# Two-layer encoder trunk on one core: accumulating transfers planned later, four products moved among the first retention tiles, and a ring of its own for results

## The chip, the core and the metric

The kernel runs on one core of one Trainium2 chip. The metric is the device time of one execution in microseconds (us). Three runs of the kernel before took 1896.23, 1899.14 and 1902.46 us, so the median is 1899.14 us. The execution under the profiler took 1899.7 us; the span from its first to its last instruction is 1897.9 us, and its mean granted TensorE clock is 0.988.

Engines are called as the profile calls them: PE (TensorE matmul), PEld (its weight loads), DVE (VectorE), ACT (ScalarE), POOL (GpSimd) and SP (SyncE, which issues most transfers).

## What is computed

Two groups of 512 rows of width 1024 pass the same two layers and a final norm. Layer 0 is differential attention, layer 1 is bidirectional retention. The change lies where layer 1's projections end, and in retention itself:

```python
def bidir_retention(h, w_in, decay_fwd, decay_bwd, subln_g, w_out):
    proj = h @ w_in
    q, k, v, gate = jnp.split(proj, [RET_QK_WIDTH, 2 * RET_QK_WIDTH, 2 * RET_QK_WIDTH + D_INNER], axis=-1)
    q = retention_rotate(q.reshape(B, S, N_HEADS, RET_QK_DIM))
    k = retention_rotate(k.reshape(B, S, N_HEADS, RET_QK_DIM)) * (RET_QK_DIM ** -0.5)
    ...
    o = rms_norm(o_f + o_b, subln_g, SUBLN_EPS)
    o = o.reshape(B, S, D_INNER) * jax.nn.silu(gate)
    return o @ w_out
...
x = x + bidir_retention(h, ret_w_in[j], ret_decay_fwd[j], ret_decay_bwd[j], ret_subln_g[j], ret_w_out[j])
...
return rms_norm(x, final_norm_g, NORM_EPS)
```

There are 8 heads; a head's output is 256 wide. Matrices are float32, and each matmul is made as three passes over a high and a low part (`PASSES`).

## The kernel before

**Plan.** Each operation is recorded by `plan.op` with its engine, an assumed cost and what it reads and writes. `Plan.arrange` then walks through an assumed course of the five engines and fixes one order for each. An operation becomes ready when the last one it depends on is done; of the ready ones an engine takes the most urgent. The order is fixed in the program, so on the chip each engine takes its instructions strictly in that order, and an instruction that waits holds everything behind it on its engine.

**Projections.** Both layers' input projections and retention's output projection are made by a seven-product scheme: P1, P2, P5, P6, P3, P7, P4 (`SEQ`) stand for the eight block products of a 2 by 2 matrix product. A `Unit` of the second projections ("pair") makes seven such products of 12 matmuls each (line 623); `projections` is a generator that gives one product per step. The products collect in three kinds of PSUM banks, x, y and z; z lies in the two banks tagged `sc`, which the retention scores use as well.

**Retention.** It runs over 16 blocks (head and group) of 4 tiles of 128 rows, 64 tiles in all, here called tile 0 to tile 63. Block after block, a tile takes these steps:

- a *score* of the next block (three matmuls, line 1222). DVE multiplies it with the decay table F (line 1226) and ACT and DVE split it into high and low part (lines 433 and 436).
- *av*: 12 matmuls into one of the two banks tagged `o` (line 1240).
- the *norm*: ACT squares and sums the result (line 785), two small POOL operations make the factor (lines 789 and 790), and ACT applies it (line 799).
- the *turn*: two PE transposes into the same bank (line 805), after which DVE multiplies with the gate (line 1291) and the bank is free for the tile after next.

On PE, av of tile i+1 stands ahead of the turn of tile i, and the turn of tile i ahead of av of tile i+2. As a tile is turned, `fill` puts two products of the output projection (`out2`, line 1347, six matmuls each) between.

**Output projection.** For each pair of heads p (0 to 3) and group g there are 14 products: seven for each of two row blocks r. For p below 3, `evac_add` forms 256 KB results in tiles tagged `out`, and `dma_add` (line 1262) adds them to the residual rows in DRAM with an accumulating transfer on POOL's queue: 48 such *pieces* (`x` in the profile). For the last p, `evac_last` adds in on-chip memory, and half sums and the final norm follow.

**Weights of the next pair.** `w_split` makes the seven operands while the second group of a pair runs. P1, P2 and P3 are loaded by SP. P5, P6 and P4 add a further 512 KB block onto P1's place `wa`, and P7 adds one onto P3's place `wb`, each with an accumulating transfer on POOL's queue: 16 such *weight blocks* (`b<-in_ret_w_out_dram` on POOL). They are called W5, W6, W7 and W4 here. Each can go only when the operand before it on its place is split (ACT line 433, DVE line 436, 128 by 1024), and is itself split when it has landed. The first pair's blocks go at the end of the projections (the *junction*); the other three sets at the three *boundaries* between pairs.

So POOL's one queue holds the small norm operations of all tiles, the weight blocks and the pieces, in one fixed order.

**Places.** Score products (`rt`), results (`out`) and the scratch of the half sums (`jk`) all take the next of eight 512-wide tiles e0 to e7 in turn. `LATE` names places for retention by hand; `turns` goes round such a list.

Of the kernel before, what the change touches and what calls it, by code (L numbers as in the profile page):

```python
# [15 lines left out]
P = 128  # L16
# [13 lines left out]
ENGINES = ("PE", "ACT", "DVE", "POOL", "SP")  # L30
PASSES = ((0, 0), (0, 1), (1, 0))
WS_BUFS = 7
LAG = 4


# [32 lines left out]
class Plan:  # L68
# [6 lines left out]
    AHEAD = 15.0  # L75

    def __init__(self):
        self.rings, self.state, self.ops, self.places = {}, {}, [], []

    def op(self, eng, cost, fn, r=(), w=(), lands=0.0, kb=0, load=False):  # L80


        n = len(self.ops)
        costs = eng if isinstance(eng, dict) else {eng: cost}
        preds, order = set(), set()
        for keys, writes in ((r, False), (w, True)):
            keys = [key if isinstance(key, tuple) else (key, None) for key in keys]
            for thing, part in keys:
                parts = self.state.setdefault(id(thing), {"thing": thing})
                if isinstance(thing, Buf):  # L90
                    if thing.nth + thing.bufs < len(thing.ring):
                        late = thing.ring[thing.nth + thing.bufs]
                        assert late.first is None, f"{thing.tag} {thing.nth} is used after its place was taken"
                    if thing.first is None:
                        assert writes, f"{thing.tag} is read before it is written"
                        thing.first = n
                        if thing.nth:
                            before = thing.ring[thing.nth - 1].first
                            assert before is not None, f"{thing.tag}: places are taken out of turn"
                            order.add(before)  # L100
                        if thing.nth >= thing.bufs:
                            preds.update(thing.ring[thing.nth - thing.bufs].users)
                        if thing.at:
                            lo, hi = thing.at
                            for b in [b for b in self.places if b.at[0] < hi and lo < b.at[1]]:
                                preds.update(b.users)
                                b.taken = True
                                self.places.remove(b)
                            self.places.append(thing)
                    elif thing.first != n:  # L110
                        assert not thing.taken, f"{thing.tag} {thing.nth} is used after its place was taken"
                        order.add(thing.first)
                    thing.users.append(n)
                for q, entry in parts.items():
                    if q == "thing" or not (part is None or q is None or q == part):
                        continue
                    if entry[0] is not None:
                        preds.add(entry[0])
                    if writes:
                        preds.update(entry[1])  # L120
                if writes:
                    if part is None:
                        for q in [q for q in parts if q != "thing"]:
                            del parts[q]
                    parts[part] = [n, []]
                else:
                    parts.setdefault(part, [None, []])[1].append(n)
        preds.discard(n)
        order -= preds
        self.ops.append((costs, fn, sorted(preds), sorted(order), lands, kb, load))  # L130
        return n

    def arrange(self, starts):
# [42 lines left out]
        while len(out) < n_ops:  # L176
            best = None
            for e in ENGINES:
                while soon[e] and (done[soon[e][0][1]] or soon[e][0][0] <= free[e]):
                    _, n = heapq.heappop(soon[e])  # L180
                    if not done[n]:
                        heapq.heappush(avail[e], (place[n] if e == "PE" else late[n], n))
                while avail[e] and done[avail[e][0][1]]:
                    heapq.heappop(avail[e])
                at = None
                if avail[e] and not (e == "PE" and avail[e][0][0] > head + self.WINDOW):
                    at = free[e]
                    if e == "SP" and ops[avail[e][0][1]][6] and avail[e][0][0] + drift - self.AHEAD > at:
                        at = avail[e][0][0] + drift - self.AHEAD
                        if soon[e]:  # L190
                            at = min(at, soon[e][0][0])
                elif soon[e]:
                    at = soon[e][0][0]
                if at is not None and (best is None or at < best[0]):
                    best = (at, e)
            assert best is not None, "stuck"
            at, e = best
            if at > free[e]:
                free[e] = at
# [12 lines left out]
            if e == "PE":  # L212
                drift = at - starts[n]
                while head < len(pe) and done[pe[head]]:
                    head += 1
            for s in succs[n]:
                same = not kb and e in ops[s][0] and len(ops[s][0]) == 1
                after = at + cost if same else end
                if n in ops[s][3]:
                    after = at  # L220
                ready[s] = max(ready[s], after)
                left[s] -= 1
                if not left[s]:
                    known(s)
# [24 lines left out]
def trunk_kernel(  # L249
# [75 lines left out]
    def place(name, shape, dt=F32, size=1024, pool=None):  # L325
# [3 lines left out]

        def make(i):  # L330
            t = (pool or wk).tile([P, size], dt, tag=name, name=label, bufs=1)
            return shaped(t[0:shape[0], 0:n], shape)
        return Buf(plan, name, 1, make, lambda i: where(name))

    def late(kind, i, shape, dt=F32):

        name = LATE[kind][i]
        if isinstance(name, int):
            return slot(name, shape, dt)
        return place(name, shape, dt, 512 if name[0] in "cm" else 1024)  # L340

    def turns(kind, shape, dt=F32):

# [5 lines left out]
    LATE = dict(q0=["raw0"], k0=["raw1"], v0=["raw2", "raw3"], aT0=["st0", "st1", "st2", "os0"], sg0=["os1"], F0=["os2"],  # L349
                aT1=[0, 1, 2, 3], k1=[4], q1=[5], v1=[6, 7], AB=[8, 9, 10], sg1=[12], F1=[13], wa=[20], wb=[21], S4=[22],  # L350
                w=[11, 14, 15, 16, 17, 18, 19, "ws5", "ws6", 23, 24, 25, 26, 27],
                AS=["ws0", "ws1", "ws2", "ws3", "ws4"], O=["m0", "m1", "m2"], R=["m3", "c3"],
                x=[20, 21, "raw0", "raw1", "raw2", "raw3", "os1", "os2"])

    def const(shape, tag, dt=F32):
        return Buf(plan, tag, 1, lambda i: view(cp, tag, i, math.prod(shape[1:]), shape, dt), lambda i: where(tag))
# [186 lines left out]
    class Unit:  # L543
        def __init__(self, w, c0, kind, done, view=None):
# [4 lines left out]
            self.wide = kind == "wide"  # L549
            self.n_ws = 2 if self.wide else 1  # L550
            self.early = None
            self.ops, self.x, self.s = {}, {}, {}
            self.banks = {}

# [55 lines left out]
        def product(self, op):  # L610
# [1 line left out]
            n_banks = 2 if self.wide else 1  # L612
            opens = op in OPENS
            if opens:
                self.banks[which] = [bank(dict(x="pj", z="sc", y="o")[which], which) for _ in range(n_banks)]
            a, b = self.ops.pop(op), B_OF[op]
            bt = [Bop[b, k] for k in range(4)]
            reads = [q[1] for q in a] + bt
# [545 lines left out]
    tab2 = load_tab(rot_tab)  # L1164
    second_units = units2(tab2)
    step(made, 4)
    proj = projections(second_units, 12)
    step(proj, 6)
    run(made)
    run(proj)  # L1170


    blocks = [(2 * p + i, g) for p in range(NH // 2) for g in range(NG) for i in range(2)]
# [41 lines left out]
    def score2(b, j):  # L1215
# [5 lines left out]
            for i, (u, v) in enumerate(PASSES):  # L1221
                nc.tensor.matmul(s.t, k[:, u, j * P:(j + 1) * P], q[:, v, :], start=(i == 0), stop=(i == 2))  # L1222
        pe(0.7, fn, [q, k], [s])
        t1 = e_t("rt")
        F = Fs[h]
        dve(S, lambda: nc.vector.tensor_tensor(t1.t, s.t, F[:, 384 - P * j:896 - P * j], op=ALU.mult), [s, F], [t1])  # L1226
        aT = late(f"aT{b % 2}", j, [P, 2, S], F32R)
# [30 lines left out]
    wop, R_, AB, AS, O2, xh, banks = {}, {}, {}, {}, {}, {}, {}  # L1258
    wa = {}

    def dma_add(out, in_, r, w, kb):
        plan.op("POOL", 1.0, lambda: nc.gpsimd.dma_start(out(), in_(), accum_op=ALU.add), r, w, lands=5.5, kb=kb)  # L1262

    def w_block(p, e, i):
        return wo2[p * S:(p + 1) * S, i * S:(i + 1) * S].rearrange("(h e p) c -> p h e c", h=2, e=2)[:, :, e, :]
# [97 lines left out]
    def evac_add(g, r, op, ps):  # L1363
# [4 lines left out]
            return c  # L1368

        def put(c, alu, t, i):  # L1370
            e = e_t("out")
            dve(S, lambda: nc.vector.tensor_tensor(e.t, c.t, ps.t, op=alu), [c, ps], [e])
            add_to(g, t, i, lambda: e.t, [e])
        if op in ("P1", "P5", "P6"):
# [5 lines left out]
        elif op == "P7":  # L1380
            put(kept["P5"], ALU.subtract, 2 + r, 1)
        else:
            e = e_t("out")
            act(S, lambda: nc.scalar.copy(e.t, ps.t), [ps], [e])
            add_to(g, 2 + r, 0, lambda: e.t, [e])

    def half_sum(g, t, i):
        ss, jk, x = col(1, "ssf", 4), e_t("jk"), xh[g, t]
        act(S + 120, lambda: nc.scalar.activation(jk.t, x[:, i * S:(i + 1) * S], AF.Square, accum_out=ss.t),
            [(x, i)], [jk, ss])  # L1390
        halves.setdefault((g, t), []).append(ss)
# [38 lines left out]
    N2 = len(tiles2)  # L1430
    owed.clear()
    fetch_sg(0)
    for op in SEQ:
        w_split(0, op)
    for j in range(NT):
        score2(0, j)
    paid = 0
    for i in range(N2 + 2):
        if i < N2:
            b, t = tiles2[i]  # L1440
            if b + 1 < NB:
# [72 lines left out]
```

## Time and profile before

| | before |
|---|---|
| median of three runs | 1899.14 us |
| profiled execution | 1899.7 us |
| its span | 1897.9 us |
| DVE busy | 1463.5 us (77%) |
| ACT busy | 966.7 us (51%) |
| POOL busy | 226.6 us (12%) |
| transfers, mean | 172 GB/s |

The second projections end at about 1525 us, and retention fills the rest. A row of the timeline gives the start, the duration, the engine, the line and the operation, then the tile written and read, and in brackets how long the engine had been idle before it and what ended that. A row of the table of windows gives, for a stretch, each engine's busy time with its count of instructions, the granted TensorE clock (1.00 is full), the share of the DMA engines' time, and GB/s. A row of transfers gives their count, the size and the time from issue to landing.

### The profile page before, as it was taken

Reading aid. Unit: us, or ns where it says so; the run is one execution under the profiler, and the core shown is the slowest. Engines: PE = TensorE matmul, PEld = TensorE weight load, DVE = VectorE, ACT = ScalarE, POOL = GpSimd, SP = SyncE. Lnnn points to the kernel's source line nnn. Section 1 sums busy time; section 2 is a strip of 40 time slices with the busy share of each in tenths; the row PEclk is TensorE's granted clock in tenths of the full one; section 3 lists DMA queues with packets and bytes.
Section 4 is the critical chain, followed back from the end, with each engine's and each line's share of the span. In section 5 each row is a group of like instructions: output and inputs, shape, how many; then the busy total and the mean of one; then the engine's idle time right before and its main releaser. Section 6 shows DMA issues by size and latency. Waiting matters only on the chain. (4 is left out here: it accounts for less than half of the span.)

```text
span 1897.9 us, 27938 instructions
## 1 busy us (share of the span) xinstructions
PE 1819.4 (96%) x10241; PEld 1569.4 (83%) x10241; DVE 1463.5 (77%) x2451; ACT 966.7 (51%) x1973; POOL 226.6 (12%) x436
## 2 busy tenths in 40 slices
PE   6999999999999899999999999999999979797987
PEld 5888988989889788888888788989898958686866
DVE  7979688688788588888887978685858477576667
ACT  6634443443444465555556754343434356455553
POOL 2000000000000011111112100000000023334332
PEclk9999999999999999999999999999999989999999
DMA  4435535545455774444453244544444688879883
GB/s 157 125 119 180 179 119 183 162 130 170 151 160 163 275 277 173 159 158 166 178 178 120 103 133 133 179 151 160 145 160 144 220 251 224 212 215 201 238 201 120
DMA packets 161025, 326.18 MB, mean 172 GB/s; under 512 B 13028, under 2 KB 73080, under 8 KB 160888
## 3 DMA queue, kind: packets, MB, share of 16 engines
q1 hardware_dynamic: 149440, 303.36, 47.9%
q0 software_dynamic: 11264, 20.98, 6.8%
q8 instruction: 80, 1.31, 0.3%
q14 instruction: 57, 0.47, 0.1%
q10 hardware_dynamic: 184, 0.08, 0.0%
HBM read 202.72 MB, written 121.63 MB: 171 GB/s over the span
## 5 line engine op out<-in xcount | busy, mean ns | idle before, releaser
L623 PE MATMUL bank<-arena,ws 128*128 128x512 f32 x2160 | 514.4, 392 | 4.9 <-DVE e L491 3.0
L623 PEld LDWEIGHTS bank<-arena,ws 128*128 128x128 f32 x2160 | 404.1, 188 | 92.9 <-ACT ws L433 3.0
L623 PE MATMUL bank<-b,ws 128*128 128x512 f32 x1200 | 293.7, 392 | 2.4 <-DVE e L660 2.4
L623 PEld LDWEIGHTS bank<-b,ws 128*128 128x128 f32 x1200 | 224.6, 188 | 51.7 <-DVE e L660 2.2
L436 DVE TENSOR_TENSOR ws<-st,ws 128x512 fp32r<-128x512 f32 (+1 forms) x192 | 147.8, 774 | 90.8 <-ACT ws L433 59.2
L652 ACT COPY c<-bank 128x512 f32<-128x512 f32 x168 | 98.2, 585 | 213.5 <-PE bank L623 134.4
L630 PE MATMUL bank<-ws,arena 128*128 128x256 f32 x1728 | 204.0, 276 | 0.0
L630 PEld LDWEIGHTS bank<-ws,arena 128*128 128x128 f32 x1728 | 201.0, 188 | 1.4
L874 PE MATMUL bank<-ws,arena 128*128 128x512 f32 x768 | 202.0, 400 | 0.0
L436 DVE TENSOR_TENSOR ws<-raw,ws 128x512 fp32r<-128x512 f32 (+1 forms) x156 | 127.4, 822 | 77.9 <-ACT ws L433 69.1
L433 ACT CAST ws<-st 128x512 fp32r<-128x512 f32 (+1 forms) x192 | 131.9, 693 | 98.5 <-PE bank L623 57.3
L789 POOL TENSOR_SCALAR css<-css 128x1 f32<-128x1 f32 x128 | 47.2, 369 | 996.3 <-ACT bank L787 918.5
L874 PEld LDWEIGHTS bank<-ws,arena 128*128 128x128 f32 x768 | 139.5, 188 | 27.2 <-ACT m L418 0.2
L433 ACT CAST ws<-raw 128x512 fp32r<-128x512 f32 (+1 forms) x156 | 114.1, 738 | 75.5 <-PE bank L623 58.8
L660 DVE TENSOR_TENSOR e<-bank,c 128x512 f32<-128x512 f32 x168 | 115.1, 685 | 32.7 <-PE bank L623 28.3
L630 PE MATMUL bank<-ws,b 128*128 128x256 f32 x960 | 116.8, 276 | 0.0
L1073 ACT ACTIVATE b<-bank,nm 128x512 f32<-128x512 f32 x128 | 88.1, 688 | 50.5 <-DVE nm L1065 50.4
L630 PEld LDWEIGHTS bank<-ws,b 128*128 128x128 f32 x960 | 113.2, 188 | 0.7
L879 DVE TENSOR_TENSOR b<-bank,b 128x512 f32<-128x512 f32 x128 | 87.7, 685 | 31.1 <-PE bank L874 29.8
L1109 PE MATMUL bank<-arena 128*128 128x256 f32 x768 | 106.5, 288 | 0.0
L1057 PE MATMUL bank<-arena 128*128 128x512 f32 x384 | 100.6, 398 | 5.0 <-ACT b L1073 5.0
L1065 DVE TENSOR_REDUCE nm<-bank 128x1 f32<-128x512 f32 x128 | 86.6, 687 | 12.5 <-PE bank L1057 12.1
(156 smaller groups left out, 2832.1 us busy)
## 6 DMA issues: line engine op xcount, KB each, us to landing
qk<-os SPq DMA_DIRECT2D x192, 256.0 KB, 3.8
arena<-qk SPq DMA_DIRECT2D x80, 512.0 KB, 4.8
raw<-in_da_w_in_dram SPq DMA_DIRECT2D x64, 512.0 KB, 4.8
v<-os SPq DMA_DIRECT2D x64, 512.0 KB, 4.1
arena<-v SPq DMA_DIRECT2D x48, 512.0 KB, 4.2
raw<-in_ret_w_in_dram SPq DMA_DIRECT2D x48, 512.0 KB, 4.4
g<-e SPq DMA_DIRECT2D x48, 256.0 KB, 4.5
x<-e POOLq DMA_DIRECT2D x48, 256.0 KB, 6.7
```

Source lines behind the costliest of these rows:

```text
L433: act(n, lambda: nc.scalar.copy(dst(), src()), r, w)
L436: dve(n, lambda: nc.vector.tensor_tensor(dst(), src(), hi().bitcast(F32), op=ALU.subtract), r, w)
L623: nc.tensor.matmul(ps.t, a[u][0]()[:, k, :], bt[k][:, v, :], start=(opens and k == 0 and i == 0), stop=(k == 3 and i == 2), skip_group_che ...
L630: nc.tensor.matmul(ps[:, (t % 2) * 256:(t % 2) * 256 + 256], bt[k][:, v, t * P:(t + 1) * P], a[u][0]()[:, k, :], start=(opens and t % 2 == ...
L652: act(S, lambda c=c, ps=ps: nc.scalar.copy(c.t, ps.t), [ps], [c])
L660: dve(S, lambda e=e, ps=ps, c=c: nc.vector.tensor_tensor(e.t, ps.t, c.t, op=ALU.add), [ps, c], [e])
L874: nc.tensor.matmul(ps.t, o[a][:, e, t * P:(t + 1) * P], u[b][:, e, :], start=(n == 0), stop=(n == 5))
L879: dve(S, lambda: nc.vector.tensor_tensor(half, ps.t, half, op=ALU.add), [ps, (x, i)], [(x, i)])
L1057: nc.tensor.matmul(s.t, q[:, a, t * P:(t + 1) * P], k[:, b, :], start=(n == 0), stop=(n == 2))
L1065: dve(S, lambda s=s, m=m: nc.vector.tensor_reduce(m.t, s.t, op=ALU.max, axis=AX.X, negate=True), [s], [m])
L1073: act(840, lambda j=j, s=s, m=m: nc.scalar.activation(p[:, j, :], s.t, AF.Exp, bias=m.t, accum_out=sm[:, j:j + 1]), [s, m], [(p, j), (sm, j)])
L1109: nc.tensor.matmul(o[:, 0:256], aT[:, a, j * P:(j + 1) * P], v[b][:, j, :], start=(n == 0), stop=(n == 11))
```

## The change

It has three parts.

1. `dma_add` carries `hold=5.0`: in the plan's assumed course an accumulating transfer is ready only 5 us after what it depends on. The 5 us is in no instruction: on the chip there is only the order that follows from it.
2. `LEFT = 4`: the last four products of the last unit (P6, P3, P7, P4) are recorded among the first retention tiles, and the first pair's `w_split` behind them. The last unit's z bank is the one tagged `tp` in place of `sc`.
3. Score products take turns over e0 to e2 and results over e3 to e7, and a few other places are exchanged: `O`, `R` and the order in `x`, where the last pair's residual rows lie.

```diff
@@ Plan
-    def op(self, eng, cost, fn, r=(), w=(), lands=0.0, kb=0, load=False):
+    def op(self, eng, cost, fn, r=(), w=(), lands=0.0, kb=0, load=False, hold=0.0):
...
+        if hold:
+            self.holds[n] = hold
...
-                ready[s] = max(ready[s], after)
+                ready[s] = max(ready[s], after + self.holds.get(s, 0.0))
@@ LATE
-                AS=["ws0", "ws1", "ws2", "ws3", "ws4"], O=["m0", "m1", "m2"], R=["m3", "c3"],
-                x=[20, 21, "raw0", "raw1", "raw2", "raw3", "os1", "os2"])
+                AS=["ws0", "ws1", "ws2", "ws3", "ws4"], O=["m1", "m2", "m3"], rt=["e0", "e1", "e2"], out=["e3", "e4", "e5", "e6", "e7"], R=["m0", "c3"],
+                x=["raw0", "raw1", 20, 21, "raw2", "raw3", "os1", "os2"])
@@ Unit
+            self.z = "sc"
...
-                self.banks[which] = [bank(dict(x="pj", z="sc", y="o")[which], which) for _ in range(n_banks)]
+                self.banks[which] = [bank(dict(x="pj", z=self.z, y="o")[which], which) for _ in range(n_banks)]
@@ trunk_kernel
+    second_units[-1].z = "tp"
...
-    run(proj)
+    step(proj, 7 * len(second_units) - 6 - LEFT)
...
-        t1 = e_t("rt")
+        t1 = turns("rt", [P, S])
...
-    def dma_add(out, in_, r, w, kb):
-        plan.op("POOL", 1.0, lambda: nc.gpsimd.dma_start(out(), in_(), accum_op=ALU.add), r, w, lands=5.5, kb=kb)
+    def dma_add(out, in_, r, w, kb, hold=5.0):
+        plan.op("POOL", 1.0, lambda: nc.gpsimd.dma_start(out(), in_(), accum_op=ALU.add), r, w, lands=5.5, kb=kb, hold=hold)
...
-            e = e_t("out")
+            e = turns("out", [P, S])
...
-    for op in SEQ:
-        w_split(0, op)
     for j in range(NT):
         score2(0, j)
-    paid = 0
     for i in range(N2 + 2):
+        if i < LEFT:
+            step(proj)
+        elif i == LEFT:
+            run(proj)
+            for op in SEQ:
+                w_split(0, op)
```

What it moves is seen in the engines' orders. In the rows of the changed kernel line 1268 is before's 1262, 794 and 795 are 789 and 790, 628 is 623, 1228 is 1222 and 810 is 805.

POOL at the first boundary, before. The rows are W5, two pieces, the norm of tile 21 (two rows), W6, the norm of tile 22, a piece, W7, a piece, and the first row of the norm of tile 23:

```order
L1262 DMA b_180_13757<-in_ret_w_out_dram 128x2x512
L1262 DMA x12_194<-e_0_432 128x512
L1262 DMA x11_193<-e_2_482 128x512
L789 TENSOR_SCALAR css_1_5427<-css_1_5427 128x1
L790 TENSOR_TENSOR crs_1_5439<-css_1_5427,mhalf_0_208 128x1
L1262 DMA b_180_13757<-in_ret_w_out_dram 128x2x512
L789 TENSOR_SCALAR css_2_5476<-css_2_5476 128x1
L790 TENSOR_TENSOR crs_2_5487<-css_2_5476,mhalf_0_208 128x1
L1262 DMA x11_193<-e_4_656 128x512
L1262 DMA b_191_13968<-in_ret_w_out_dram 128x2x512
L1262 DMA x13_195<-e_6_705 128x512
L789 TENSOR_SCALAR css_3_5531<-css_3_5531 128x1
```

The same place in the changed kernel, some rows further on: a piece, W7 (`b_231`), the norm of tile 24, W6 (`b_216`), two pieces, and the norm of tile 25:

```order
L1268 DMA x11_193<-b_234_14050 128x512
L1268 DMA b_231_14004<-in_ret_w_out_dram 128x2x512
L794 TENSOR_SCALAR css_0_5375<-css_0_5375 128x1
L795 TENSOR_TENSOR crs_0_5388<-css_0_5375,mhalf_0_208 128x1
L1268 DMA b_216_13784<-in_ret_w_out_dram 128x2x512
L1268 DMA x13_195<-b_239_14089 128x512
L1268 DMA x13_195<-b_244_14129 128x512
L794 TENSOR_SCALAR css_1_5427<-css_1_5427 128x1
L795 TENSOR_TENSOR crs_1_5439<-css_1_5427,mhalf_0_208 128x1
```

So W7 moved ahead of W6 and behind the norm of tile 23, with one norm between the two blocks, and W6 has two pieces right behind it. Ahead of these rows the changed order reads: a piece, W5, the norm of tile 21, two pieces, the norms of tiles 22 and 23. The same pattern stands at all three boundaries, on both sides.

POOL at the junction, in the changed kernel: the norm of tile 5, W7, the norm of tile 6, W6, the norm of tile 7. (Before, W5 stood ahead of every norm, W6 behind the norm of tile 2, W7 behind that of tile 3, and the norm of tile 4 behind W7.)

```order
L794 TENSOR_SCALAR css_1_5427<-css_1_5427 128x1
L795 TENSOR_TENSOR crs_1_5439<-css_1_5427,mhalf_0_208 128x1
L1268 DMA b_134_13096<-in_ret_w_out_dram 128x2x512
L794 TENSOR_SCALAR css_2_5476<-css_2_5476 128x1
L795 TENSOR_TENSOR crs_2_5487<-css_2_5476,mhalf_0_208 128x1
L1268 DMA b_131_12988<-in_ret_w_out_dram 128x2x512
L794 TENSOR_SCALAR css_3_5531<-css_3_5531 128x1
L795 TENSOR_TENSOR crs_3_5542<-css_3_5531,mhalf_0_208 128x1
```

W5 now stands behind the norm of tile 1 and W4 behind that of tile 10 (before: tile 5), so each weight block stands two to five tiles later.

PE at the junction, before: the end of P7, two scores, P4 (four rows that collect in `bank_2`), four scores.

```order
L623 MATMUL bank_2_393<-b_100_9427,ws_2_356 128x512 x3
L1222 MATMUL bank_4_303<-b_105_12810,b_106_12813 128x512 x3
L1222 MATMUL bank_3_289<-b_105_12810,b_106_12813 128x512 x3
L623 MATMUL bank_2_393<-b_101_9473,ws_3_408 128x512 x3
L623 MATMUL bank_2_393<-b_102_9489,ws_3_408 128x512 x3
L623 MATMUL bank_2_393<-b_103_9492,ws_3_408 128x512 x3
L623 MATMUL bank_2_393<-b_104_9495,ws_3_408 128x512 x3
L1222 MATMUL bank_4_303<-b_105_12810,b_106_12813 128x512 x3
L1222 MATMUL bank_3_289<-b_105_12810,b_106_12813 128x512 x3
L1222 MATMUL bank_4_303<-arena_75 128x512 x3
L1222 MATMUL bank_3_289<-arena_75 128x512 x3
```

In the changed kernel the first two scores stand ahead of P6, P3 and P7, and P4 stands behind av of tile 1 and one more score, ahead of the turns of tiles 0 and 1:

```order
L1228 MATMUL bank_3_289<-arena_75 128x512 x3
L628 MATMUL bank_2_393<-b_101_9473,ws_3_408 128x512 x3
L628 MATMUL bank_2_393<-b_102_9489,ws_3_408 128x512 x3
L628 MATMUL bank_2_393<-b_103_9492,ws_3_408 128x512 x3
L628 MATMUL bank_2_393<-b_104_9495,ws_3_408 128x512 x3
L810 MATMUL bank_5_282<-ident_0_212,on_0_206 128x128 x2
L810 MATMUL bank_6_296<-ident_0_212,on_1_5212 128x128 x2
```

Up to P5 of the last unit PE's order is the same in both kernels.

More of the change, by code (lines that the diff above doesn't have):

```diff
@@ L32 @@
 WS_BUFS = 7
+LEFT = 4
 LAG = 4
@@ L77, in __init__ @@
     def __init__(self):
-        self.rings, self.state, self.ops, self.places = {}, {}, [], []
-    def op(self, eng, cost, fn, r=(), w=(), lands=0.0, kb=0, load=False):
+        self.rings, self.state, self.ops, self.places, self.holds = {}, {}, [], [], {}
+    def op(self, eng, cost, fn, r=(), w=(), lands=0.0, kb=0, load=False, hold=0.0):
         n = len(self.ops)
@@ L331, in make @@
             t = (pool or wk).tile([P, size], dt, tag=name, name=label, bufs=1)
+            places.pop((name.rstrip("0123456789"), int(name.lstrip("abcdefghijklmnopqrstuvwxyz"))), None)
             return shaped(t[0:shape[0], 0:n], shape)
@@ L339, in late @@
             return slot(name, shape, dt)
-        return place(name, shape, dt, 512 if name[0] in "cm" else 1024)
+        return place(name, shape, dt, 512 if name[0] in "cme" else 1024)
     def turns(kind, shape, dt=F32):
@@ L1382, in evac_add @@
         else:
-            e = e_t("out")
+            e = turns("out", [P, S])
             act(S, lambda: nc.scalar.copy(e.t, ps.t), [ps], [e])
@@ L1387, in half_sum @@
     def half_sum(g, t, i):
-        ss, jk, x = col(1, "ssf", 4), e_t("jk"), xh[g, t]
+        ss, jk, x = col(1, "ssf", 4), turns("out", [P, S]), xh[g, t]
         act(S + 120, lambda: nc.scalar.activation(jk.t, x[:, i * S:(i + 1) * S], AF.Square, accum_out=ss.t),
```

## The prediction

> **What bounds the kernel now.** The page's first section says which engine to look at.
>
> ```profile
> PE 1819.4 (96%) x10241; PEld 1569.4 (83%) x10241; DVE 1463.5 (77%) x2451; ACT 966.7 (51%) x1973; POOL 226.6 (12%) x436
> ```
>
> PE is busy for 1819.4 of 1897.9 us, and the change neither adds nor removes a matmul. So it can only win or lose in PE's idle time, 78.5 us, and in time at a lowered clock. The table of windows over the stages that the change touches shows where that time lies.
>
> ```profile
> 1520.00:1550.00 30.00, 22.61 (x131) 18.37 (x129) 27.71 (x50) 20.90 (x44) 6.87 (x10) 1.00 0.94 297
> 1550.00:1570.00 20.00, 13.75 (x64) 12.21 (x65) 10.15 (x18) 11.30 (x26) 7.99 (x12) 0.66 0.67 164
> 1570.00:1630.00 60.00, 60.00 (x350) 52.24 (x349) 42.91 (x85) 35.84 (x87) 23.23 (x38) 1.00 0.82 221
> 1630.00:1660.00 30.00, 19.35 (x99) 15.55 (x98) 15.27 (x26) 12.71 (x28) 12.76 (x17) 0.89 0.91 210
> 1720.00:1750.00 30.00, 19.62 (x103) 15.81 (x102) 15.84 (x27) 13.29 (x29) 12.80 (x17) 0.89 0.94 210
> 1810.00:1840.00 30.00, 21.32 (x105) 16.72 (x104) 17.31 (x30) 14.23 (x31) 11.87 (x17) 0.91 0.85 187
> 1840.00:1898.00 58.00, 47.95 (x242) 38.81 (x240) 42.75 (x74) 22.66 (x64) 13.22 (x28) 0.94 0.41 145
> ```
>
> Between the boundaries PE is full (60.00 of 60). At the junction it idles 7.39 + 6.25 us, at the three boundaries 10.65, 10.38 and 8.68, and at the end 10.05. The waits of PE in the first boundary say for what.
>
> ```profile
> 1635.19 0.44 PE L805 MATMUL bank<-ident,on 128*128 128x128 f32 x2 [1.41 <-ACT on L799]
> 1636.92 1.66 PE L1347 MATMUL bank<-b,b 128*128 128x512 f32 x6 [0.60 <-ACT c L1367]
> 1639.22 1.69 PE L1240 MATMUL bank<-arena 128*128 128x256 f32 x12 [0.64 <-DVE b L1291]
> 1641.90 0.44 PE L805 MATMUL bank<-ident,on 128*128 128x128 f32 x2 [0.99 <-ACT on L799]
> 1644.26 1.59 PE L1240 MATMUL bank<-b,b 128*128 128x256 f32 x12
> 1652.87 0.69 PE L805 MATMUL bank<-ident,on 128*128 128x128 f32 x2 [7.02 <-ACT on L799]
> ```
>
> A turn waits for the applied norm, most of all 7.02 us for tile 23. ACT in its turn waited for POOL, and POOL's own rows, with two of ACT's, show why:
>
> ```profile
> 1624.52 1.26 POOL L1262 DMA_DIRECT2D b<-in_ret_w_out_dram  x1 [0.71 <-DVE b L1291]
> 1625.80 0.94 POOL L1262 DMA_DIRECT2D x<-e  x1
> 1632.80 0.89 POOL L1262 DMA_DIRECT2D x<-e  x1 [6.07 <-issue]
> 1641.30 0.94 POOL L1262 DMA_DIRECT2D x<-e  x1
> 1644.49 1.25 POOL L1262 DMA_DIRECT2D b<-in_ret_w_out_dram  x1 [2.25 <-DVE b L1291]
> 1650.45 0.92 POOL L1262 DMA_DIRECT2D x<-e  x1 [4.71 <-issue]
> 1651.07 0.59 POOL L789 TENSOR_SCALAR css<-css 128x1 f32<-128x1 f32 x1
> ...
> 1642.56 0.37 ACT L785 ACTIVATE bank<-bank 128x256 f32<-128x256 f32 x1
> 1652.35 0.47 ACT L799 ACTIVATE on<-bank,crs 128x256 f32<-128x256 f32 x1 [7.10 <-POOL crs L790]
> ```
>
> Tile 23 was squared at 1642.56, but its norm started at 1651.07, behind a piece that POOL could not start before 1650.45. The views of transfers, in windows around single issues, give what such a piece waits for: the landing of an earlier one.
>
> ```profile
> b<-in_ret_w_out_dram POOLq DMA_DIRECT2D x1, 512.0 KB, 8.0
> x<-e POOLq DMA_DIRECT2D x1, 256.0 KB, 8.3
> ...
> b<-in_ret_w_out_dram POOLq DMA_DIRECT2D x1, 512.0 KB, 8.9
> x<-e POOLq DMA_DIRECT2D x1, 256.0 KB, 8.8
> ...
> b<-in_ret_w_out_dram POOLq DMA_DIRECT2D x1, 512.0 KB, 6.1
> ...
> b<-in_ret_w_out_dram POOLq DMA_DIRECT2D x16, 512.0 KB, 6.8
> ```
>
> The block of 1624.52 landed 8.0 us later, at 1632.52, and the piece started at 1632.80. The piece of 1641.30 took 8.8, until 1650.10, and the next one started at 1650.45. (The 8.9 is W7 of 1644.49, the 6.1 W6 of 1638.06, the last row the page's median.) I read a limit from this: **one weight block and one piece can be under way; a second piece or block starts 0.3 us after the earliest has landed**, and all norms behind it wait. At the junction two blocks collide in the same way:
>
> ```profile
> 1541.70 1.29 POOL L1262 DMA_DIRECT2D b<-in_ret_w_out_dram  x1 [1.06 <-DVE arena L436]
> 1552.90 1.25 POOL L1262 DMA_DIRECT2D b<-in_ret_w_out_dram  x1 [8.75 <-issue]
> ...
> b<-in_ret_w_out_dram POOLq DMA_DIRECT2D x1, 512.0 KB, 10.9
> ...
> 1555.66 0.69 PE L805 MATMUL bank<-ident,on 128*128 128x128 f32 x2 [7.42 <-ACT on L799]
> ```
>
> W6 landed at 1552.60, W7 started at 1552.90, the norm of tile 4 stood behind it, and its turn 2.76 us after W7's start.
>
> **The junction.** In the changed order W6 stands behind W7 with one norm between, so the collision remains, but with tile 7's norm behind it. From tile 5's norm to the turn of tile 7 PE has more to do than before: 1.8 us from norm to turn (1651.07 to 1652.87), then the turn of tile 5, av of 7, the turn of 6, a product, av of 8, a product. By the rows of normal tiles these are 0.38 + 1.44 + 0.38 + 1.4 + 1.44 + 1.4, some 6.2 us net of overlap:
>
> ```profile
> 1599.16 0.38 PE L805 MATMUL bank<-ident,on 128*128 128x128 f32 x2
> 1602.88 0.38 PE L805 MATMUL bank<-ident,on 128*128 128x128 f32 x2
> 1607.99 0.38 PE L805 MATMUL bank<-ident,on 128*128 128x128 f32 x2
> ```
>
> (3.72 us is a turn, a score, a product and an av; 5.11 is that and a second product.) W7 starts 0.6 behind the norm's start, W6 a landing L plus 0.3 later, and the turn 2.76 after that. So 0.6 + L + 0.3 + 2.76 - 8.0 = L - 4.3 remains of the 7.42. At the median of 6.8 this is 2.5 (4.9 won), at 5.6 it is 1.3, at 10.9 it is 6.6 (0.8 won). A wait of 2.5 also spares the clock: 0.66 was granted in 1550 to 1570, while the short waits of 1520 to 1550 left it at 1.00. The slowed rows there cost some 3.7 us (two av took 2.76 and 2.93 in place of 1.6; a score and a product the rest). That would be 8.6 in all.
>
> The other 7.39 us stay, in my view. DVE is busy 27.71 of 30 us there, since the first scores can't be evacuated before the table F has landed (1520.2). Moving scores ahead of P6 and P4 behind two avs fills PE's gaps with work, but it takes nothing from DVE. Scores 0 and 1 are now early and wait for F as before. DVE also caps the gain: 27.71 + 10.15 = 37.86 us of work at the pace of 27.71 in 30 need 41.0 of the 50 us, so at most 9.0 can go. Between 0.8 and 9.0 I take **7.5**, near the 8.6.
>
> **The boundaries.** The piece behind W5 no longer stops a norm for long: tile 21's norm now stands ahead of the two pieces. So the 1.41 + 0.60 + 0.64 + 0.99 = 3.64 us ahead of the big wait go. But a worse group follows: W7, norm 24, W6, two pieces, norm 25. By the limit W6 waits until W7 has landed (L1), and the second piece until W6 has (L2). The times: tile 23 is squared at 1642.56 - 3.64 = 1638.9; square 0.5, norm 0.9, piece 0.95, so W7 goes at 1641.2. The second piece starts at 1641.2 + L1 + 0.3 + L2 + 0.3, and a turn follows the start of a piece ahead of its norm by 2.42 (1650.45 to 1652.87): tile 25 is turned at 1644.2 + L1 + L2. PE would be there when av of tile 24 (1644.26) is done 1.44 later, less 3.64: 1642.06; from there a long and a short stretch of tiles, 5.11 + 3.72, give 1650.9. The new wait is **L1 + L2 - 6.7**. For L1 I take 7.5, between 6.1 (W6, issued alone 3.5 us earlier in the same traffic) and 8.9 (W7), for L2 the median 6.8: a wait of 7.6. Against 10.65, 10.38 and 8.68 this wins 3.05, 2.8 and 1.1, in sum **7.0**. At 5.6 twice (the shortest block I found) it is 4.5 each and 16.2 won; at 8.9 + 8.0 it is 10.2 each and 0.9 lost. The lowered clock behind the wait (0.89 before) stays.
>
> A rule of the Trainium skill speaks against a wait of this size. Its page "DMA: Bandwidth & Descriptors", section "Anatomy of one DMA — SWDGE (gpsimd) path", gives a transfer on this path about 2.0 us and its bytes over 436e3 per us; for 512 KB that is an estimate of 3.2 us. By it L1 + L2 would be 6.4, no wait would be left, and the sum would be the second rival's. The trace differs: its 16 blocks, which add to what they find, have a median of 6.8.
>
> **The rest.** The rings for `rt` and `out` cost nothing: a place in `out` returns after five results, some 25 us, and a piece is under way for 6.7 (page) and blocked for up to 15. At the end, W4 of the last pair now stands behind a row norm of the last products, and two residual rows lie in `wa` and `wb` and load after it. PE has some 14 us of other work listed there; I take 0, and from -3 to +3 as bounds.
>
> **The sum.** 1899.7 - 7.5 - 7.0 = 1885.2; the profiled execution is 0.6 above the median of the runs, so 1885 us. Bounds: 1899.7 - 9.0 - 16.2 - 3 = 1871.5, and 1899.7 - 0.8 + 0.9 + 3 = 1902.8.
>
> **Rivals.**
> - *The wait only moves.* Landings of 8.3 at both places give L1 + L2 = 16.6, 9.9 us at each boundary as before, and 4.0 left at the junction: 3.4 won, 1896. For it: each boundary still has two blocks and three pieces on one queue. Against it: 3.64 us of small waits go in any case.
> - *No wait is left.* If the limit is not what I read, or landings are so short that L1 + L2 is below 6.7, the whole of 10.65 + 10.38 + 8.68 = 29.7 goes, the clock behind it (1.8 each) and 9.0 at the junction: about 1856. Against it: 11.2 is the least that the rows allow.
> - *Two blocks and two pieces in a row are worse than what they replace.* If the DMA engines, at 0.91 of their time in a boundary, land both blocks in the 10.9 of the junction's W6, each wait is 15.1: 45.3 for 29.7, and 0.8 won at the junction: 1914. It decides from L1 + L2 = 18.7, where the loss is 5.7 us. Against it: 10.9 was seen once in 16.
>
> **How the numbers follow.** A measurement of this kernel tells about 0.3% (5.7 us) from no change. My forecast, 1885, has 0.60; the moved wait 0.20; no wait 0.08; the slower case 0.12. So faster 0.68, same 0.20, slower 0.12. The range, 1871 to 1898, holds the forecast with its bounds and most of the moved wait.
>
> **What would show it.** In the changed profile: at the junction a wait of 1 to 7 us before tile 7's turn, and a granted clock near 1.00 in 1550 to 1570. At each boundary no wait before the turns of tiles 21 to 23, and one of 5 to 10 us before tile 25's, with POOL's second piece starting 0.3 us after W6's landing. Between boundaries PE stays full. A norm that waits nowhere would prove the limit wrong; a wait that starts earlier, or DVE idle for F for longer, my junction.

## The result, and the profile after

Twelve executions of each kernel: **1891.46 us** median (1884.92 to 1896.61) after the change, 1899.78 us (1896.23 to 1906.03) before it; the ratio is 0.995, with a 95% interval of 0.9934 to 0.9966. The forecast was 1885, in 1871 to 1898: a gain of some 8 to 9 us where 14 were forecast. The profiled execution took 1895.15 us, 3.7 above the median of its kernel.

In the changed kernel the lines that matter stand 5 or 6 further down: L1268 is the accumulating transfer, L810 the turn, L804 the applied norm, L790 and L794 the square and the POOL norm, L1246 av, L1297 the gate, L1353 the output projection. First its page, span and busy times, then its table of windows over the stages shown before. In a row of windows PE's busy time is the second number, the granted clock the third from the end.

```profile
span 1893.4 us, 27928 instructions
...
PE 1823.2 (96%) x10241; PEld 1574.5 (83%) x10241; DVE 1462.6 (77%) x2451; ACT 967.5 (51%) x1973; POOL 230.8 (12%) x436
```

```profile
1520.00:1550.00 30.00, 26.24 (x140) 21.77 (x139) 22.88 (x42) 20.35 (x44) 6.20 (x11) 0.94 0.81 275
1550.00:1570.00 20.00, 16.85 (x100) 13.84 (x100) 17.20 (x32) 12.99 (x31) 9.38 (x12) 1.00 0.95 282
1570.00:1630.00 60.00, 58.41 (x341) 50.71 (x340) 43.52 (x85) 36.83 (x88) 26.57 (x40) 1.00 0.83 216
1630.00:1660.00 30.00, 21.72 (x115) 18.15 (x115) 16.65 (x31) 13.69 (x31) 10.10 (x15) 0.87 0.83 203
1720.00:1750.00 30.00, 19.94 (x106) 17.16 (x105) 16.70 (x31) 13.55 (x31) 9.12 (x12) 0.85 0.77 185
1810.00:1840.00 30.00, 20.41 (x107) 17.22 (x106) 17.20 (x30) 13.96 (x31) 10.25 (x14) 0.83 0.81 187
```

At the junction (first three rows) PE idles 3.76 + 3.15 + 1.59 = 8.50 us, where it idled 13.64. At the boundaries it idles 8.28, 10.06 and 9.59 us, where it idled 10.65, 10.38 and 8.68: nearly as much as before. The granted clock is 1.00 in 1550 to 1570, where it was 0.66, but 0.94 in 1520 to 1550, where it was 1.00.

**Where the time went, place by place.** The spans differ by 4.5 us, but that isn't the change's worth: the changed execution was already behind when it came to the first moved instruction. Rows of the two timelines at places with the same work ahead of them show it: an ACT row ahead of the change, the turn of tile 14 behind the junction (before, at 1599.16), and the turns of tiles 29 and 45 behind the first and the second boundary. The kernel before comes first, then the changed one.

```profile
1452.02 0.63 ACT L728 ACTIVATE c<-e 128x512 f32<-128x512 f32 x1 [0.88 <-DVE e L660]
1685.56 0.38 PE L805 MATMUL bank<-ident,on 128*128 128x128 f32 x2
1774.90 0.38 PE L805 MATMUL bank<-ident,on 128*128 128x128 f32 x2
```

```profile
1456.45 0.64 ACT L733 ACTIVATE c<-e 128x512 f32<-128x512 f32 x1 [0.88 <-DVE e L665]
1597.00 0.38 PE L810 MATMUL bank<-ident,on 128*128 128x128 f32 x2
1681.12 0.38 PE L810 MATMUL bank<-ident,on 128*128 128x128 f32 x2
1770.21 0.38 PE L810 MATMUL bank<-ident,on 128*128 128x128 f32 x2
```

| place | changed less before, us | won since the place above, us |
|---|---|---|
| ahead of the change | +4.43 | |
| tile 14, behind the junction | -2.16 | 6.59 |
| tile 29, behind boundary 1 | -4.44 | 2.28 |
| tile 45, behind boundary 2 | -4.69 | 0.25 |
| end of the span | -4.5 | -0.2 |

So the changed part won 8.9 us in this execution, about what the medians show (8.3). Two further profiles of the same kernel, reckoned in the same way, give 8.9 us each; their junctions won 5.1 and 5.7 us where this one won 6.6. (The third boundary has no row of its own: behind it the changed kernel has moved two products of the output projection to a later place, so the rows there do not have the same work ahead of them.)

**The waits that are left.** PE's rows with the large waits in the changed kernel, at the junction and at the three boundaries:

```profile
1563.97 0.44 PE L810 MATMUL bank<-ident,on 128*128 128x128 f32 x2 [1.27 <-ACT on L804]
1590.35 1.70 PE L1246 MATMUL bank<-arena 128*128 128x256 f32 x12 [1.59 <-DVE b L1297]
1656.53 0.69 PE L810 MATMUL bank<-ident,on 128*128 128x128 f32 x2 [7.86 <-ACT on L804]
1745.84 0.69 PE L810 MATMUL bank<-ident,on 128*128 128x128 f32 x2 [10.06 <-ACT on L804]
1834.82 0.69 PE L810 MATMUL bank<-ident,on 128*128 128x128 f32 x2 [9.18 <-ACT on L804]
```

Tile 7's turn waits 1.27 us. At each boundary one large wait is left, before the turn of tile 25 (41, 57) and no longer of tile 23. POOL's rows in the first boundary show why, and behind them the transfers issued at 1638.11 and 1638.73 (a piece and W7), and at 1648.04 (W6), with the time to landing at the end:

```profile
1638.11 0.93 POOL L1268 DMA_DIRECT2D x<-b  x1
1638.73 1.57 POOL L1268 DMA_DIRECT2D b<-in_ret_w_out_dram  x1
1640.41 0.22 POOL L794 TENSOR_SCALAR css<-css 128x1 f32<-128x1 f32 x1
1648.04 1.27 POOL L1268 DMA_DIRECT2D b<-in_ret_w_out_dram  x1 [6.76 <-DVE og L1209]
1648.81 1.45 POOL L1268 DMA_DIRECT2D x<-b  x1
1654.16 0.86 POOL L1268 DMA_DIRECT2D x<-b  x1 [3.90 <-issue]
1654.75 0.56 POOL L794 TENSOR_SCALAR css<-css 128x1 f32<-128x1 f32 x1
```

```profile
b<-in_ret_w_out_dram POOLq DMA_DIRECT2D x1, 512.0 KB, 9.0
x<-b POOLq DMA_DIRECT2D x1, 256.0 KB, 5.7
...
b<-in_ret_w_out_dram POOLq DMA_DIRECT2D x1, 512.0 KB, 5.8
```

W7 lands at 1638.73 + 9.0 = 1647.73, and W6 starts at 1648.04, 0.31 later; W6 lands at 1648.04 + 5.8 = 1653.84, and the second piece starts at 1654.16, 0.32 later; tile 25's norm follows at once. ACT has no work in between: it waits 9.45 us for that norm. (The row of 1648.04 names a DVE result as what ended the wait. With the landing 0.31 us ahead of it, as at every other such place, I take the landing.)

What went over the DMA queues while W7 was under way (1638.73 to 1647.73), and then while W6 was (1648.04 to 1653.84), is this; the columns are packets, MB and the share of the 16 engines' time, the hardware queue is SP's and the software queue POOL's:

```profile
q1 hardware_dynamic: 523, 1.81, 52.1%
q0 software_dynamic: 416, 0.79, 47.9%
...
q0 software_dynamic: 323, 0.63, 69.2%
```

So W7 had a piece ahead of it and 1.81 MB of SP's transfers beside it. W6 had none of SP's, and landed in 5.8 us although a piece was issued 0.77 us behind it.

### The profile page after: what moved, and what is told of

It is laid out like the page before. It is cut to its first block, busy times and chain, and to the rows that moved or that the text cites. A ratio compares the mean times of both kernels' runs of the same rounds, so it can differ in the third digit from the quotient of the medians.

```text
span 1893.4 us, 27928 instructions
## 1 busy us (share of the span) xinstructions
PE 1823.2 (96%) x10241; PEld 1574.5 (83%) x10241; DVE 1462.6 (77%) x2451; ACT 967.5 (51%) x1973; POOL 230.8 (12%) x436
## 4 chain that ended last, share of the span: by engine, by line
PE 83%; DVE 6%; issue 3%; DMA 3%; ACT 3%; POOL 2%; SPq 0%; POOLq 0%; DVEq 0%; ACTq 0%
PE bank L628 36%; PE bank L635 16%; PE bank L879 8%; PE bank L1353 5%; PE bank L1114 5%; PE bank L1062 4%; PE bank L1246 3%; PE bank L1228 2%; PE bank L1098 1%; PE bank L810 1%; DMA b<-in_dist_dram 1%; DVE arena L440 1%; DVE b L440 1%; DMA b<-in_ret_w_out_dram 1%; DVE ws L440 1%
## 5 line engine op out<-in xcount | busy, mean ns | idle before, releaser
L794 POOL TENSOR_SCALAR css<-css 128x1 f32<-128x1 f32 x128 | 46.0, 359 | 1522.7 <-ACT bank L792 924.1
L1070 DVE TENSOR_REDUCE nm<-bank 128x1 f32<-128x512 f32 x128 | 86.6, 687 | 12.6 <-PE bank L1062 12.2
```

## The experiments

Open work is counted in *units* in what follows: 17 for a weight block and 9 for a piece, for 256 and 128 rows of 2 KB over 16 DMA engines, and one more. The Trainium skill, "DMA: Bandwidth & Descriptors", section "The descriptor swizzle", has such a closing entry on each engine for a transfer of 1 MiB to 128 partitions. No run here shows the entry: counts of 16 and 8 would fit the runs as well. That `dynamic_dma_scratch_size` is the memory for the descriptors of this queue is my reading of its name. Medians are of 4 to 12 executions, and each ratio is taken to executions of the kernel before in the same session (medians of 1899.05 to 1900.71 us). The changes behind the names:

```diff
# after_room, before_room, late_products_room, hold_3_room: on the changed kernel, the one before, no_hold and hold_3
-    nc = _bacc.Bacc("TRN2", ..., dynamic_dma_scratch_size=1024)
+    nc = _bacc.Bacc("TRN2", ..., dynamic_dma_scratch_size=1536)
# no_hold (0.0), hold_3 (3.0); rings_alone has no_hold's and no_late_products' edits
-    def dma_add(out, in_, r, w, kb, hold=5.0):
+    def dma_add(out, in_, r, w, kb, hold=0.0):
# no_late_products
-    second_units[-1].z = "tp"
-    step(proj, 7 * len(second_units) - 6 - LEFT)
+    run(proj)
+    for op in SEQ:
+        w_split(0, op)
```

### Is it room on the queue?

> The changed kernel, with the memory that POOL's queue has for descriptors raised from 1024 to 1536 bytes a partition, and nothing else: the same order on every engine. Theory A (a transfer that would pass a fixed amount of open work on the queue holds POOL up until the oldest has landed): the amount goes from between 27 and 34 units (a weight block 17, a piece 9) to between 40 and 51, so the second block of a boundary starts without a wait or behind a piece, the second piece behind the first block, some 6 us earlier. The waits of 7.86, 10.06 and 9.18 us fall to 0 to 3 each, tile 7's 1.27 goes: 1870 us (1865 to 1876). Theory B (a transfer on this queue can't start before the one ahead has landed, whatever room there is, or the DMA engines at 0.8 of their time are what holds it): the waits stay within 1 us, and 1891. Theory C (POOL no longer stops, but blocks in the air together land later, and products wait for them): half of it, 1880.

> The kernel before, with the same 1536 bytes and nothing else. Theory A: at the junction the block behind W6 starts at once and the wait of 7.42 us before tile 4's turn goes, with the lowered clock behind it; the boundaries keep some 3 us each of their 10.65, 10.38 and 8.68: 1899.8 - 7.4 - 3 - 20 = 1869 (1865 to 1880). If that comes out, the change's moves buy little that room doesn't buy alone. Theory B: 1900.

| | median, us | ratio to before (95%) |
|---|---|---|
| after_room | 1877.6 | 0.9883 (0.9866 to 0.9901) |
| before_room | 1883.03 | 0.9913 (0.9893 to 0.9932) |

With the same order on every engine, 512 bytes more a partition won 14 us on the changed kernel and 16 on the kernel before, about twice what the change did: theory B falls. POOL's rows of after_room at the same place, and PE's row of tile 25's turn:

```profile
1641.43 1.57 POOL L1268 DMA_DIRECT2D b<-in_ret_w_out_dram  x1
1644.10 1.25 POOL L1268 DMA_DIRECT2D b<-in_ret_w_out_dram  x1
1648.19 0.93 POOL L1268 DMA_DIRECT2D x<-b  x1 [2.84 <-issue]
1651.73 0.87 POOL L1268 DMA_DIRECT2D x<-b  x1 [2.61 <-issue]
...
1654.11 0.44 PE L810 MATMUL bank<-ident,on 128*128 128x128 f32 x2 [2.73 <-ACT on L804]
```

W6 now starts 2.67 us behind W7, not 9.31. It brings the open work to 43 units, which passes; a piece more would be 52, and that waits. The turn waits 2.73 us, 3.00 and 3.16 at the other boundaries, as theory A had it. Over the four kernels with room, 44 units were under way at most and 52 never; with 1024 bytes, 27 at most, and 34 or 35 never. Half as much again as 27 to 34 is 40 to 51, which fits 44 to 52: the limit grew with the memory.

The sums were off all the same, 1877.6 for 1870 and 1883 for 1869, both outside theory A's ranges; 1877.6 lies nearer to theory C's 1880. In after_room two blocks in the air together landed in 10.0 and 9.9 us: theory C's part. In before_room PE idled 5.46, 4.63 and 7.37 us at the boundaries, where I had put 3 each: its order asks for 52 units there, and pieces with norms behind them waited for the raised limit too. And the junction kept 4.68 us, which POOL's queue no longer makes:

```profile
1553.10 1.04 ACT L433 CAST arena<-b 128x1024 fp32r<-128x1024 f32 x1 [5.25 <-DMA b<-in_ret_w_out_dram]
1554.05 0.37 ACT L785 ACTIVATE bank<-bank 128x256 f32<-128x256 f32 x1
...
1556.73 0.69 PE L805 MATMUL bank<-ident,on 128*128 128x128 f32 x2 [4.68 <-ACT on L799]
```

ACT's split of W6 (128x1024) waits for the landing, and the square for tile 5's norm stands behind it on ACT (tile 4's wait of 7.42 is gone). I had not reckoned with that: the block's landing holds up a norm by a second way.

### Which part of the change wins what?

> The changed kernel without the holding back: the four late products and the rings alone. On POOL each boundary then has a block, a norm and a block as before. My account (in the profiled pair the junction won 6.6 of 9.0 us, the boundaries 2.3): the junction's win stays, the boundaries' waits add to some 28 to 32 us: 1893 (1890 to 1896). Rival (the holding back is what won): 1898 to 1900.

> The changed kernel with the second projections ended ahead of retention's first tiles as before: the holding back and the rings alone. Boundaries as in the changed kernel (one wait of 8 to 10 us each); at the junction two blocks stand with one norm between them, right behind tile 4's norm, and hold up tile 6's: a wait of 3 to 7 us, and DVE's 7.39 us as before. My account: 2 to 5 us of the gain left, 1895 to 1898. Rival (the holding back is what won): 1891 to 1893.

> The changed kernel without late products and without holding back: the own rings for results, score rows and final pieces, and the places of the pieces, alone. My account: its queue on POOL reads as before but for the last block of a pair, which comes one norm later, so the waits stay and it is 1899 (1896 to 1901); late products and holding back then win 3.9 and 5.4 us each of their own. Rival (the rings give part of no_hold's and no_late_products' gains): 1896 or less.

| | median, us | ratio to before (95%) |
|---|---|---|
| no_hold | 1895.18 | 0.9983 (0.9965 to 1.0) |
| no_late_products | 1893.7 | 0.9972 (0.9957 to 0.9987) |
| rings_alone | 1898.6 | 0.9994 (0.9978 to 1.001) |

The rings are worth nothing that can be measured. No_hold came out inside its range, but not for my reason: the junction's large wait is still there.

```profile
1548.46 0.69 PE L810 MATMUL bank<-ident,on 128*128 128x128 f32 x2 [6.82 <-ACT on L804]
```

With holding back alone, the largest wait before a turn at the junction is this one:

```profile
1560.13 0.44 PE L810 MATMUL bank<-ident,on 128*128 128x128 f32 x2 [2.36 <-ACT on L804]
```

With and without holding back, two blocks stand on POOL with one norm between them. What differs is where they stand, and how long the first takes to land. In no_hold it goes at 1535.04 and lands in 10.4 us; in the changed kernel it goes at 1554.11 and lands in 5.8. SP's queue in these two stretches, no_hold first:

```profile
q1 hardware_dynamic: 904, 2.81, 76.1%
...
q1 hardware_dynamic: 176, 0.64, 29.0%
```

That the later place wins because SP moves less beside the block fits these figures; no run tests it alone. Reckoned by place as above, one profile each, the junction won 2.1 us in no_hold and 4.5 in no_late_products, against 5.1 to 6.6 with both. So the junction's gain, which I had put down to the late products, looks to be more the holding back's. No_late_products came out at 1893.7, between my account's range and the rival's. The intervals of the two parts overlap. By the medians each alone wins less than both together (0.9950), but no_late_products' interval reaches into that of both; how the gain is shared is not settled beyond that.

### Another order, and both

> The changed kernel with transfers held back 3 in place of 5 in the planner's time; 1024 bytes as in the changed kernel. On POOL a boundary then reads block, piece, norm, piece, norm, piece, norm, block, piece, norm, block, piece, norm: no two blocks have a norm and then two pieces behind them. Theory A (room on the queue): behind the third block stand only one piece and a norm, which wait for one landing and not for two, behind a block that starts about a tile earlier: 1 to 5 us of wait at each boundary in place of 8 to 10, so 1891.5 - 15 = 1876 (1871 to 1882). Rival (what counts is the work on the queue in a boundary, wherever it stands): 1891.

> hold_3 once more, for the same question. Theory P: 279 ns, and 1882 (1877 to 1886). Theory E: 276 or 277 more likely than not.

> hold_3 with 1536 bytes: both. Theory A, with blocks in the air together landing in 10 us: nothing passes the raised amount for long at a boundary, and no norm waits there, so after_room's 2.7 to 3.2 us at each boundary go as well: 1877.6 - 8 = 1869 (1866 to 1874). Rival (the rest of after_room's waits isn't POOL's queue): 1877.

> hold_3_room once more: is the fastest version that fast again? 1867 (1863 to 1872). Theory P: 277 ns as in its first profile, since it is the same program; theory E: either.

> no_hold with 1536 bytes: the four late products and the rings, no holding back, and room. Theory A: it differs from before_room (1883.0) at the junction alone, where before_room still waits 4.69 us for a second block: 3 to 8 us won, 1877 (1874 to 1881), so that with room the holding back is worth 0 to 4 us. Rival (holding back is worth as much with room as without): 1882 or above.

| | median, us | ratio to before (95%) |
|---|---|---|
| hold_3 | 1882.71 | 0.9909 (0.9891 to 0.9927) |
| hold_3_again | 1882.52 | 0.9894 (0.9863 to 0.9926) |
| hold_3_room | 1865.42 | 0.9838 (0.9813 to 0.9863) |
| hold_3_room_again | 1869.21 | 0.9838 (0.9811 to 0.9865) |
| late_products_room | 1874.78 | 0.9872 (0.985 to 0.9894) |

A hold of 3 in place of 5, with no more room, wins 9 us on the changed kernel, so the rival falls: with the same work in a boundary, what stands behind what decides. PE's rows of hold_3 at tile 25's turn and the av behind it:

```profile
1649.52 0.44 PE L810 MATMUL bank<-ident,on 128*128 128x128 f32 x2 [0.62 <-ACT on L804]
...
1654.14 2.60 PE L1246 MATMUL bank<-b,b 128*128 128x256 f32 x12 [2.10 <-DVE b L1297]
```

The turn's wait of 7.86 is 0.62 here. I had forecast 15 us, in 1871 to 1882, and 1882.7 and 1882.5 are just outside. What is left are mostly waits for gates and for splits of blocks that land late, 0.6 to 2.5 us each (one of 3.75 in the second profile). With room as well it is the fastest kernel of the study, 1.6% below the one before and 22 to 26 us below the changed one. In its first boundary PE is busy for 27.94 of 30 us at full clock, and the waits that are left are short ones on splits and gates:

```profile
1630.00:1660.00 30.00, 27.94 (x159) 23.64 (x158) 22.92 (x44) 19.37 (x44) 14.89 (x19) 1.00 1.06 273
...
1642.05 0.50 PE L1353 MATMUL bank<-b,b 128*128 128x512 f32 x1 [0.76 <-DVE b L440]
1647.21 1.70 PE L1246 MATMUL bank<-b,b 128*128 128x256 f32 x12 [1.30 <-DVE b L1297]
```

Late_products_room, without any holding back, can't be told from after_room: given room, a hold of 5 is worth nothing that shows, and one of 3 some 6 to 9 us by the medians, with intervals that still meet.

### The 4.43 us ahead of the change

> The changed kernel once more, for the 4.43 us by which its profiled execution was behind the one of before ahead of the first moved instruction. Theory P (it belongs to the program, by where its instructions lie): the same steps at 38, 195 to 218, 330 to 354, 464 to 488 and 598 to 621 us, again 3.9 to 4.9 us in sum at 1490. Theory E (it belongs to the execution): another sum, from -5 to +5, at other places. Waits at the boundaries 7 to 11 us each again, and 1891 (1886 to 1896).

> The changed kernel a third time, for the products of 256 columns ahead of the changed place: a mean of 279 ns in the changed kernel (twice), with room, and with the hold of 3; 276 or 277 in five others. Theory P (it goes with the program): 279 again, and steps of 1.47 us at 195 to 218, 330 to 354, 464 to 488 and 598 to 621. Theory E (it goes with the execution): 4 of 9 profiles had it, so 276 or 277 more likely than not.

They gave 1890.62 us (0.9955; 0.9938 to 0.9971) and 1891.99 (0.9954; 0.9936 to 0.9972). The groups of the projections' products of 256 columns, in the changed kernel's first profile and then in its third (mean ns at the end of the busy column):

```profile
L635 PE MATMUL bank<-ws,arena 128*128 128x256 f32 x1728 | 207.7, 279 | 0.0
L635 PE MATMUL bank<-ws,b 128*128 128x256 f32 x960 | 118.9, 279 | 0.0
```

```profile
L635 PE MATMUL bank<-ws,arena 128*128 128x256 f32 x1728 | 204.0, 276 | 0.0
L635 PE MATMUL bank<-ws,b 128*128 128x256 f32 x960 | 116.8, 276 | 0.0
```

For the same program the two columns add to 326.6 us for these 2688 products once and to 320.8 another time, 5.8 us apart, so it goes with the execution and not with the program: theory P falls. With such and smaller steps, the profiled executions stand between 4.2 us ahead of the one of before and 4.5 us behind it at the place where the change begins. Hold_3, run twice, showed both values too. What sets it stays open.

## Why the prediction was right, and where it was off

- **The limit on POOL's queue** holds. W6 and the second piece start 0.3 us behind a landing, and the memory for descriptors moves the limit. Read in units it is wider than the prediction had it: three pieces (27) also pass.
- **The junction**: 7.5 us forecast, 6.6 measured (5.1 and 5.7 in the other two profiles). Tile 7's turn waits 1.27 us; L - 4.3 at W7's landing of 5.8 is 1.5. The granted clock in 1550 to 1570 is 1.00, as forecast, but 1520 to 1550 fell to 0.94, which the forecast left out. DVE's waits stayed, and grew a little later: the 1.59 us at 1590 is new. The formula held. But the prediction had no reason why W7 should land early there: it took the median of 6.8, got 5.8, and would have kept most of the wait with the 10.4 of no_hold, so this part is in some measure luck. That the late products win the junction is not borne out by no_hold.
- **The small waits at the first boundary** (3.64 us) are gone but for 0.42 us, as forecast.
- **The new wait before tile 25's turn** was right in its place and its formula, and wrong in one size. L1 + L2 - 6.7 with the landings of the trace (9.0 + 5.8, 11.0 + 6.1, 10.2 + 6.0) gives 8.1, 10.4 and 9.5 us; measured were 7.86, 10.06 and 9.18. I had taken 7.5 for L1 and 6.8 for L2, a wait of 7.6 at each. **The mis-sized term is L1, 10.1 on the mean.** Over the three boundaries it came out 7.7 us longer than forecast, and L2 2.5 us shorter; that makes up the boundaries' shortfall: 2.3 us won with the end, 7.0 forecast. It came of taking the landing as a property of the block. In the changed kernel eight blocks that went with nothing else open on POOL's queue landed in 5.8 to 7.6 us, seven of them in at most 6.1; eight that went behind an open piece took 6.4 to 11.0, with a median of 9.25. W7 goes 0.6 us behind a piece, and the kernel before showed the pair already: 8.9 for its W7 behind a piece, 6.1 for its W6 alone. But the piece is not shown to be the cause. In the kernel before a block that went alone, at the junction, took 10.9, and four behind a piece took 6.0 to 6.9; and W7 has 1.81 MB of SP's transfers beside it. What the piece and what SP's transfers add is not separated by any run.
- **The short estimate.** The 3.2 us for 512 KB, estimated from the Trainium skill ("DMA: Bandwidth & Descriptors", section "Anatomy of one DMA — SWDGE (gpsimd) path"), do not meet these transfers: the shortest of the changed kernel's 16 blocks took 5.8.
- **The end** and the third boundary together won nothing (-0.2), where 0 and 1.1 were forecast; they can't be told apart.
- **The range.** It is said to hold the forecast with its bounds, but its upper end, 1898, lies below the bound of 1902.8 that the sum gives. The result fell inside both.
- **The rivals.** *The wait only moves* is what happened at the second and third boundary, where it put 9.9 us; the junction's gain kept the sum from that rival's 1896. L1 + L2 came out as 14.8, 17.1 and 16.2, two of the three nearer to that rival's 16.6 than to my 14.3, and 1891.5 lies a little nearer to its 1896 than to 1885. Neither of the other two came.

## What to carry to other kernels

POOL's queue of accumulating transfers has room here for a set amount of open work: count what is open at each issue, and look what else stands behind it in that engine's order, before moving transfers about. A cure that needed no new order was 512 bytes a partition of memory for descriptors, and order and memory together won more than three times what the change did. Don't price a transfer by its size alone: look at what is under way beside it, on SP's queue as well. And count the worth of a change from the first moved instruction on, since two executions may be several us apart before that.

## What was not expected of the hardware

- The limit on open accumulating transfers grew with the memory set aside for descriptors: between 27 and 34 units at 1024 bytes a partition, between 44 and 52 at 1536. The Trainium skill, "SBUF — State Buffer", section "SBUF size: 192, 224, or 256?", lists a scratch for DMA descriptors in on-chip memory, the ring buffer of this kind of transfer; that the parameter sets its size is my reading, and that a full one holds up everything behind it on POOL is what the runs add.
- The landing of a 512 KB block varies by a factor of two. Over the 14 profiles, 79 blocks that went with nothing else open on POOL's queue took 5.6 to 11.5 us (median 6.0), 102 behind one open piece 5.6 to 12.1 (median 8.7), and 16 behind an open block and a piece 9.8 to 12.6 (median 10.75).
- The same 2688 products of 256 columns take 276 to 277 or 279 ns each on the mean, in one execution or another of one program, with a granted clock of 1.00 in either.
